# Equal slots for the heads' matrices in a hybrid conv and delta-rule step, with merged inverse levels and fewer last-token transposes

## The chip, the core and the metric

The kernel runs on one core of one Trainium2 chip. The metric is the device time of one execution in microseconds, and lower is better. A core has these engines, each working through its own queue of instructions in order: TensorE (PE in the profile, with its weight loads as PEld), VectorE (DVE), ScalarE (ACT), GpSimd (POOL), and SyncE (SP), which issues most of the DMA transfers. Engines wait for each other through semaphores. SBUF is the on-chip memory of 128 partitions, PSUM holds what TensorE writes.

## The reference

One layer of a hybrid decoder works on 1024 prompt tokens and 8 sample tokens, 1032 columns in all. A normalised input goes through one input projection; branch A is a short gated convolution, branch B a gated delta rule over 8 heads in chunks of 64 tokens; both are projected, merged by sigmoid gates, and go through an output projection. Outputs are the tokens, the last rows of both convolutions, and the heads' states.

```python
h = rmsnorm(x, norm_pre) * (1.0 + scale[:, None]) + shift[:, None]
proj = h @ w_in
hA, cA, bA, zA, qkv, zB, beta_raw, alpha_raw, gA, gB = jnp.split(proj, offs, axis=-1)
a_conv, new_buf_a = causal_dwconv(cA * hA, buf_a, conv_a_w)
yA = ((bA * a_conv) * jax.nn.silu(zA)) @ w_out_a
qkv_c, new_buf_b = causal_dwconv(qkv, buf_b, conv_b_w)
...
# per head and chunk: decay = exp(gc_i - gc_j), gc the running sum of log decays
a_mat = jnp.where(strict, jnp.einsum('bhncd,bhnsd->bhncs', kb, k) * decay, 0.0)
a_mat = a_mat + jnp.eye(C, dtype=jnp.float32)
sol = lax.linalg.triangular_solve(a_mat, rhs, left_side=True, lower=True, unit_diagonal=True)
...
def step(S, xs):
    v_new = u_c - jnp.einsum('bhcd,bhde->bhce', w_c, S)
    o = jnp.einsum('bhcd,bhde->bhce', qd_c, S) + jnp.einsum('bhcs,bhse->bhce', aqk_c, v_new)
    S = S * gl_c[..., None, None] + jnp.einsum('bhcd,bhce->bhde', kd_c, v_new)
    return S, o
...
merged = jax.nn.sigmoid(gA) * yA + jax.nn.sigmoid(gB) * yB
post = rmsnorm(merged @ w_o, norm_post)
y = (x + gate[:, None] * post).astype(x.dtype)
```

## The kernel before

Every large product is made in float32 by three matmuls on split operands: the high part of the input with the high part of the weights (xh,whi), the low part of the input (xl,whi), and the low part of the weights (xh,wlo). `run` walks a list of jobs. A **job** is one block of 128 columns of the input projection: three groups of 344 tokens, in each eight times three matmuls of 128x344, 72 in all. ScalarE makes the high part of a job's weights and VectorE the low part; an `evac` takes each group out of its accumulator. The order of the program is: the start-up (norm and modulation); the jobs of the heads (columns of K, Q and V, a gate and the gate zB for each head, then the remaining gates); `products`, which makes branch A's columns by a seven-product Strassen scheme (in the order P1, P2, P6, P7, P4, P5, P3) with matmuls of 128x258 columns, from operands (tiles qa, qb, q, thi, tlo) that VectorE builds ahead; `products_b`; the jobs of the output projections; and the tail with w_o.

The heads' delta rule runs in the gaps of the heads' jobs as **strands**, Python generators that `slot` steps between wide matmuls. A model of the clocks of all engines (`Sched`) decides at which wide matmul a strand's next piece is put in: `note` prices an instruction, `dma` a transfer, and a strand is stepped once the time of its last result lies `SLK` behind TensorE's modelled clock. What is decided there is the fixed order of each engine's queue. `Slots` is a pool of equal buffers (`T4`) with `get` and `give`; `ready` tells whether some are free, and strands wait by `yield` until they are.

A head passes these stages. `decay_gen` loads the head's running sums gc, broadcast to all partitions, into gcB, subtracts the token's own (DA), and forms two matrices of exponentials, DB for the inverse and DA for q by k. `delta_gen` then transposes k (`pa_t<-ident,kq`) into kd and sums its squares, does the same sums for q, multiplies k and q by k in split form (kqh, kql) into DB and DA, transposes v into vp, and scales q by the exponential of gcB. The kernel's chunks have 128 tokens, 8 in a head. The inverse of each chunk's 128x128 triangle is found in levels: its four diagonal blocks of 32 by VectorE in Tw (Ttmp; their layout is changed by way of DRAM, sA to At and sT to Tn), then the two halves of 64 one after the other (`Un,DB`, `Qs,Tn`, `Tn,Qs`), then the whole (`U,DB` and `Qs,T`). It is put together in U, one buffer that all heads share and that is cleared once. The **scan** goes over the chunks in order: `S,kq` on TensorE, X on VectorE, `X,U`, vn on ScalarE, `vn,kd` and `vn,DA`, then the new state S on VectorE. At the end the output `on` is normalised, transposed (`pa_t<-ident,on`) and gated by sz. `sample_gen` does the sample tokens (`qs_s,S`, matmuls of 128x2). `conv_state_gen` transposes the last tokens' rows of q, k, v (last_q, 24 tiles of 11 tokens) and of branch A (last_a, 8 tiles of 10) and stores them.

The buffers of `bp` (kq with 3, DA, DB, kd and vp with 2, gcB, Tw, Tn, Un, Qs, sz with 1) tie heads to each other: `decay_gen` of head h waits for head h-1's scaled q, and for the inverse and then the whole scan of head h-2; the inverse of head h waits for the scan of head h-1 because U is shared. All instructions are recorded through one helper, so their line is that of the helper (124 before, 134 after); they are told apart by tile names.

## Time and profile before

| what | value |
|---|---|
| time, median of three runs | 1429.38 us (1427.04 to 1431.44) |
| the profiled execution's own time | 1428.2 us |
| its span, first to last instruction | 1426.1 us |
| mean granted TensorE clock | 0.995 |
| bytes moved by DMA | 161.80 MB, 113 GB/s on average |
| the most frequent matmul, xh,whi of 128x344 and 128x512 columns | 1384 times, 453.4 us |
| TensorE waiting for DVE rx_y, in the start-up | 6.3 us, once |

The span holds all instructions; 2.1 us of the execution lie around it. In the profile's groups a row reads: line, engine, operation, output from inputs (partitions by elements), count, then busy time and the mean of one in ns. In the timeline a row reads: start, duration, engine, line, operation, and in brackets the idle time before it with its releaser. Matmuls are pipelined, so the durations of neighbours overlap; their pitch is the distance of the starts. Stages by time: start-up to about 80 us, the heads' jobs to 816 us, products and products_b after that, output projections and tail at the end.

### The profile page before, as it was taken

What the parts mean: (1) busy time and instruction counts of PE and PEld (TensorE: products, weight loads), DVE (VectorE), ACT (ScalarE), POOL (GpSimd) and SP (SyncE); (2) the same over time, 40 slices, a digit from 0 to 9 for tenths busy, and PEclk for the clock granted to TensorE, in tenths of its full rate; (3) what the DMA queues carried; (4) which work ended last, traced back from release to release, by engine and by line L of the source; (5) the groups of instructions that cost most, each with busy time, mean ns of one, the idle gap of its engine ahead of it and who ended that gap; (6) DMA issues with size and microseconds to landing.
All of it is one profiled execution on the core that took longest, in us unless ns stands there. A gap on an engine that the chain in (4) does not pass through costs nothing.

```text
span 1426.1 us, 26358 instructions
## 1 busy us (share of the span) xinstructions
PE 1394.4 (98%) x10274; PEld 1328.4 (93%) x10274; DVE 990.5 (69%) x2516; ACT 674.7 (47%) x1534; POOL 31.0 (2%) x72
## 2 busy tenths in 40 slices
PE   6999999999999999999999999999999999999997
PEld 4899998999989899998999999999999999999786
DVE  6766875697758768676463988877777787854553
ACT  6756744856466555747433433333333345432211
POOL 0000000000000000000000000000000110000000
PEclk9999999999999999999899999999999999999999
DMA  9622432153412423241332465432211876752321
GB/s 321 145 48 78 118 97 72 33 125 82 108 55 70 121 51 104 68 108 56 96 104 73 133 224 178 134 90 75 61 54 59 231 225 213 239 161 86 96 85 60
DMA packets 191591, 161.80 MB, mean 113 GB/s; under 512 B 34503, under 2 KB 167008, under 8 KB 191458
## 3 DMA queue, kind: packets, MB, share of 16 engines
q1 hardware_dynamic: 186912, 151.58, 36.0%
q0 software_dynamic: 4352, 8.46, 2.1%
q8 instruction: 81, 1.33, 0.4%
q14 instruction: 44, 0.36, 0.1%
q10 hardware_dynamic: 202, 0.08, 0.0%
HBM read 123.40 MB, written 36.91 MB: 112 GB/s over the span
## 4 chain that ended last, share of the span: by engine, by line
PE 78%; DVE 10%; DMA 6%; ACT 3%; issue 2%; SPq 1%; DVEq 0%; ACTq 0%
PE pm_t L124 53%; PE pa_t L124 23%; PE pb L124 2%; DVE wlo L124 1%; DVE Ttmp L124 1%; DVE Tw L124 1%; DMA At<-sA 1%; DVE acc L124 1%; SPq L124 1%; DMA xs<-in_x_prompt_dram 1%; DMA gcB<-gsc 1%; DVE on L124 1%; DVE mrg L124 1%; DVE vT L124 1%; DVE ro_a L124 0%
## 5 line engine op out<-in xcount | busy, mean ns | idle before, releaser
L124 PE MATMUL pm_t<-xh,whi 128*128 128x344 f32 (+1 forms) x1384 | 453.4, 328 | 0.0
L124 PE MATMUL pm_t<-xl,whi 128*128 128x344 f32 (+1 forms) x1384 | 436.2, 315 | 0.0
L124 PE MATMUL pm_t<-xh,wlo 128*128 128x344 f32 (+1 forms) x1384 | 435.8, 315 | 0.0
L124 PEld LDWEIGHTS pm_t<-xh,whi 128*128 128x128 f32 x1384 | 261.6, 189 | 1.6
L124 PEld LDWEIGHTS pm_t<-xl,whi 128*128 128x128 f32 x1384 | 261.8, 189 | 0.4
L124 PEld LDWEIGHTS pm_t<-xh,wlo 128*128 128x128 f32 x1384 | 261.2, 189 | 0.4
L124 ACT CAST whi<-wr 128x1024 fp32r<-128x1024 f32 x60 | 62.8, 1047 | 139.4 <-PE pm_t L124 65.7
L124 DVE TENSOR_TENSOR wlo<-wraw,whi 128x512 fp32r<-128x512 f32 x112 | 76.5, 688 | 35.6 <-ACT whi L124 35.1
L124 ACT CAST whi<-wraw 128x512 fp32r<-128x512 f32 x112 | 68.7, 624 | 55.8 <-PE pm_t L124 53.0
L124 PE MATMUL pm_t<-thi,wlo 128*128 128x258 f32 x304 | 86.3, 284 | 1.3 <-DVE wlo L124 1.2
L124 PE MATMUL pa_t<-thi,wlo 128*128 128x258 f32 x304 | 86.2, 284 | 0.1
L124 PE MATMUL pm_t<-tlo,whi 128*128 128x258 f32 x304 | 85.9, 283 | 0.0
L124 PE MATMUL pa_t<-tlo,whi 128*128 128x258 f32 x304 | 85.9, 283 | 0.0
L124 PE MATMUL pm_t<-thi,whi 128*128 128x258 f32 x304 | 85.8, 282 | 0.0
L124 PE MATMUL pa_t<-thi,whi 128*128 128x258 f32 x304 | 85.8, 282 | 0.0
L124 DVE TENSOR_TENSOR wlo<-wr,whi 128x1024 fp32r<-128x1024 f32 x60 | 73.2, 1220 | 10.3 <-ACT whi L124 10.1
L124 PE MATMUL pa_t<-xh,whi 128*128 128x258 f32 x256 | 72.4, 283 | 0.0
L124 PE MATMUL pa_t<-xh,wlo 128*128 128x258 f32 x256 | 72.2, 282 | 0.0
L124 PE MATMUL pa_t<-xl,whi 128*128 128x258 f32 x256 | 72.2, 282 | 0.0
L124 DVE SCALAR_TENSOR_TENSOR kq<-raw,vecs,kq 128x528 f32<-128x528 f32 x96 | 69.6, 761 | 2.4 <-ACT kq L124 2.4
L124 PE MATMUL pm_t<-ylo,whi 128*128 128x344 f32 x192 | 61.4, 321 | 0.6 <-DVE ylo L124 0.6
L124 PE MATMUL pm_t<-yhi,whi 128*128 128x344 f32 x192 | 61.4, 321 | 0.0
(397 smaller groups left out, 3065.5 us busy)
## 6 DMA issues: line engine op xcount, KB each, us to landing
wraw<-in_w_in_dram SPq DMA_DIRECT2D x48, 512.0 KB
wr<-in_w_in_dram SPq DMA_DIRECT2D x64, 256.0 KB
aw<-in_ada_w_dram SPq DMA_DIRECT2D x16, 512.0 KB
gBsc<-gate SPq DMA_DIRECT2D x8, 516.0 KB
gAsc<-gate SPq DMA_DIRECT2D x8, 516.0 KB
txs<-phi SPq DMA_DIRECT2D x8, 516.0 KB
txs<-plo SPq DMA_DIRECT2D x8, 516.0 KB
yAsc<-acc SPq DMA_DIRECT2D x8, 516.0 KB
```

The lines of the kernel that those rows point to most:

```text
L124: r = f(*args, **kw)
```

## The change

Buffers: T4 has 7 slots for 6, and 11 more ("hb") that live as long as `bp`. DB, DA, kd, gcB, the inverse's small tiles (Tw, Tn, Un and Qs in one slot, Ts) and sz now take slots; vp is written over vT, `on` over DA, and U over DB, whose other blocks POOL clears (`clear`, 24 memsets). A slot carries the modelled time at which it comes free, and `ready` counts only those whose time has come. A head's decay matrices no longer wait for the scan of head h-2, nor its inverse for the scan of head h-1; the scan alone waits for the scan before it.

Loads: the gc rows are loaded once into DA and a second time into gcB, for the scaled q, which a strand of its own (`qd_gen`) now makes. q's sums move behind the transposes of v.

Levels: the two halves of 64 go out in one step. Last tokens: last_q and last_a are stored with tokens outside and tiles inside, so that three transposes (72, 96 and 96 columns) and one (80) take the place of 24 and 8; stores are cut by token. The model: a transfer issued by SyncE costs 380 ns, arrives 800 behind, and one with short runs or a broadcast costs 4.7 times its size (`spread`).

```diff
-NT4 = 6
+NT4 = 7
+NHB = 11
...
+        t = max(self.clk[eng], self.cur.t if self.cur else self.clk["PE"]) + (380.0 if eng == "SY" and not self.cold else 60.0)
...
-        self.arrival = self.clk["DMA"] + 700.0
+        self.arrival = self.clk["DMA"] + 800.0
...
+def spread(out, in_):
+    a, b = ([d for d in x.ap if d[1] > 1] for x in (out, in_))
+    run = min(x[-1][1] if x and x[-1][0] == 1 else 1 for x in (a, b))
+    return 4.7 if run <= 32 or (b and b[0][0] == 0) else 1.0
...
         def ready(self, n=1):
-            return len(self.free) >= n
+            t = max(sched.clk["PE"], sched.cur.t if sched.cur else 0.0)
+            return sum(i[3] <= t for i in self.free) >= n
...
-        def give(self, v):
-            self.free.append(self.held.pop(id(v))[0])
+        def give(self, v, t=0.0):
+            i = self.held.pop(id(v))[0]
+            self.free.append(i[:3] + (max(t, sched.cur.t if sched.cur else 0.0),))
...
+    gc_rows = lambda h: gsc.rearrange("(c h) i -> h c i", h=NH)[h].unsqueeze(0).to_broadcast([P, NC, C])
...
     def decay_gen(h, st):
-        while not flags.get("ba") or (h and not flags.get(("qd", h - 1))) \
-                or (h > 1 and not flags.get(("inv", h - 2))):
-            yield
-        gcB = bp.tile([P, NC, C], F32, tag="gcB", name="gcB")
-        SY.dma_start(out=gcB, in_=gsc.rearrange("(c h) i -> h c i", h=NH)[h].unsqueeze(0).to_broadcast([P, NC, C]))
-        yield
-        while h > 1 and not flags.get(("done", h - 2)):
-            yield
-        DB = bp.tile([P, NC, C], F32, tag="DB", name="DB", bufs=2)
-        DA = bp.tile([P, NC, C], F32, tag="DA", name="DA", bufs=2)
+        yield from when(lambda: flags.get("ba") and (not h or flags.get((DEC, h - 1))), lambda: T4.ready(RDC))
+        DB_, DA_ = (T4.get(n_, S) for n_ in ("DB", "DA"))
+        DB, DA = (v.rearrange("p (c i) -> p c i", i=C) for v in (DB_, DA_))
+        SY.dma_start(out=DA, in_=gc_rows(h))
+        yield
         for c in range(NC):
-            act(DA[:, c, :], gcB[:, c, :], AF.Identity, bias=neg["gc"][:, c, h:h + 1])
+            act(DA[:, c, :], DA[:, c, :], AF.Identity, bias=neg["gc"][:, c, h:h + 1])
...
+        st.update(DB=DB, DA=DA, DB_=DB_, DA_=DA_)
...
+    def clear(v):
+        t = sched.cur.t
+        GP.memset(v, 0.0)
+        sched.cur.t, sched.cur.eng = t, None
+
+    def qd_gen(h, qd, gcB, t):
+        sched.at(t)
+        yield
         act(gcB, gcB, AF.Exp)
-        st.update(gcB=gcB, DB=DB, DA=DA)
+        yield
+        tt(qd, qd, gcB, ALU.mult)
+        T4.give(gcB)
+        flags[("qd", h)] = True
...
-        kq, vT, gcB, DB, DA = st["kq"], st["v"], st["gcB"], st["DB"], st["DA"]
+        yield from when(lambda: "DA" in st)
+        waiting.add(h)
+        yield from when(lambda: T4.ready(RDL - 1))
+        waiting.discard(h)
+        kq, vT, DB, DA = st["kq"], st["v"], st["DB"], st["DA"]
...
+        kd_, kh_, kl_ = (T4.get(n_, S) for n_ in ("kd", "kqh", "kql"))
+        kd, vp = (v.rearrange("p (c d) -> p c d", d=C) for v in (kd_, vT[:, 0:S]))
...
-        Tw = bp.tile([P, 8, 32], F32, tag="Tw", name="Tw")
+        Tw, Tn, Un = (Ts_[:, o:o + 256].rearrange("p (r j) -> p r j", j=32) for o in (0, 512, 768))
+        Qs = Ts_[:, 0:512].rearrange("p (c j) -> p c j", j=64)
...
-        T4.give(vT)
-        qd = kq[:, 1, 0:S]
-        tt(qd, qd, gcB.rearrange("p c i -> p (c i)"), ALU.mult)
-        flags[("qd", h)] = True
-        yield
+        yield from when(lambda: T4.ready())
+        gcB = T4.get("gcB", S)
+        sched.loose()
+        SY.dma_start(out=gcB.rearrange("p (c i) -> p c i", i=C), in_=gc_rows(h))
+        t_gc = sched.arrival
+        sched.loose(False)
+        yield from sums(1, ssq)
+        start(qd_gen(h, kq[:, 1, 0:S], gcB, t_gc))
...
+        U_, U = st["DB_"], DB
...
         yield
-        while h and not flags.get(("done", h - 1)):
-            yield
...
-        for p in range(2):
-            b1 = slice(64 * p, 64 * p + 32)
-            b2 = slice(64 * p + 32, 64 * p + 64)
-            pt = ps_aux().rearrange("p (c j) -> p c j", j=64)
+        B1, B2 = ([slice(64 * p + o, 64 * p + o + 32) for p in range(2)] for o in (0, 32))
+        pt = ps_aux().rearrange("p (c j) -> p c j", j=64)
+        for b1, b2 in zip(B1, B2):
             for c in range(NC):
                 PE.matmul(pt[b1, c, 0:32], lhsT=DB[b2, c, b1], rhs=Un[b2, c, :], start=True, stop=True)
+        sched.loose()
+        for b1 in B1:
             A.copy(out=Qs[b1, :, 0:32], in_=pt[b1, :, 0:32])
-            yield
-        for p in (0, 1):
-            b1 = slice(64 * p, 64 * p + 32)
-            b2 = slice(64 * p + 32, 64 * p + 64)
-            pt = ps_aux().rearrange("p (c j) -> p c j", j=64)
+        sched.join("A")
+        yield
+        for b1, b2 in zip(B1, B2):
+            clear(U[b2, :, b1])
+        pt, pt2 = (ps_aux().rearrange("p (c j) -> p c j", j=64) for _ in range(2))
+        for b1 in B1:
             for c in range(NC):
                 PE.matmul(pt[b1, c, 0:32], lhsT=Tn[b1, c, :], rhs=Qs[b1, c, 0:32], start=True, stop=True)
...
+        for c in range(NC):
+            PE.matmul(pt2[B2[0], c, 0:32], lhsT=Qs[B1[0], c, 0:32], rhs=Tn[B1[0], c, :], start=True, stop=True)
+        sched.loose()
+        A.copy(out=U[B1[1], :, B2[1]], in_=pt[B1[1], :, 0:32])
+        A.copy(out=U[B1[0], :, B2[0]], in_=pt[B1[0], :, 0:32])
+        A.copy(out=T11[B2[0], :, 0:32], in_=pt2[B2[0], :, 0:32])
+        sched.join("A")
...
-        flags[("inv", h)] = True
+        clear(U[64:128, :, 0:64])
...
-        while (h > 1 and not flags.get(("out", h - 2))) or not T4.ready():
-            yield
...
+        T4.give(Ts_)
+        flags[("inv", h)] = True
...
+
+        on_, on = st["DA_"], DA
+        yield from when(lambda: flags.get(("qd", h)) and (not h or flags.get(("done", h - 1))))
...
+        for v in (kd_, vT, U_):
+            T4.give(v)
...
-                st["szt"] = bp.tile([P, NT], F32, tag="sz", name="sz", bufs=1)
+                st["szt"] = T4.take("sz", NT)
...
+            src, nt, o_p, o_s, row, cuts = last_q, 24, n_conv_qkv_p, n_conv_qkv_s, 2, (0, 3, 7, 11)
...
-            for t0 in range(0, nt, 4):
-                pt = ps_aux()
-                for t in range(4):
-                    transpose(pt[:n, t * P:(t + 1) * P], src[:, t0 + t, :])
-                while not T4.ready():
-                    yield
...
+            src, nt, o_p, o_s, row, cuts = last_a, NK, n_conv_a_p, n_conv_a_s, 1, (0, 10)
+        flat, np_ = src.rearrange("p n t -> p (n t)"), cuts[-1] - NB
+        groups = list(enumerate(zip(cuts, cuts[1:])))
+        yield from when(lambda: T4.ready())
+        lq = T4.get("lq", 512)
+        pt = ps_aux()
+        for g, (a, b) in groups:
+            transpose(pt[:(b - a) * nt, g * P:(g + 1) * P], flat[:, a * nt:b * nt])
...
+            if a == 0:
+                store(o_p[0, 0].rearrange("n (t d) -> (n t) d", d=P), v[:np_ * nt])
+            for n in range(max(a, np_), b):
+                store(o_s[0, n - np_, row].rearrange("(t d) -> t d", d=P), v[(n - a) * nt:(n - a + 1) * nt])
+        T4.give(lq)
```

TensorE, about the end of head 6's inverse, where before the inverse meets the last-token transposes (S_8211 is a sample state, T_ the assembled inverse; Qs and Tn belong to the halves of 64):

```order
L124 MATMUL pa_t<-ident,last_q 11x128 x4
L124 MATMUL pa_t<-Qs,Tn 32x32 x8
L124 MATMUL pa_t<-Tn,Qs 32x32 x8
L124 MATMUL pm_t<-xh,wlo 128x344
L124 MATMUL pa_t<-qs_s,S_8211 128x2 x8
L124 MATMUL pm_t<-xh,whi 128x344
L124 MATMUL pm_t<-xl,whi 128x344
L124 MATMUL pm_t<-xh,wlo 128x344
L124 MATMUL pm_t<-xh,whi 128x344
L124 MATMUL pa_t<-ident,last_q 11x128 x4
L124 MATMUL pa_t<-Qs,Tn 32x32 x8
L124 MATMUL pa_t<-ident,last_q 11x128 x4
```

Four wide matmuls in a row are the most that stand there between small groups (of four transposes, eight 32x32 or eight 128x2 matmuls). After the change the last-token transposes are gone from there. The sparsest place is now another one, 42.1 jobs into the heads' stage, where the last head's vT and the output of the head before (DA) are transposed beside the samples' matmuls:

```order
L134 MATMUL pa_t<-ident,vT 128x128 x4
L134 MATMUL pa_t<-qs_s,S_8425 128x2 x4
L134 MATMUL pm_t<-xh,whi 128x344
L134 MATMUL pm_t<-xl,whi 128x344
L134 MATMUL pm_t<-xh,wlo 128x344
L134 MATMUL pa_t<-ident,DA 128x128 x4
L134 MATMUL pa_t<-S,kq 128x128 x2
L134 MATMUL pa_t<-qs_s,S_8425 128x2 x4
L134 MATMUL pm_t<-xh,whi 128x344
L134 MATMUL pm_t<-xl,whi 128x344
L134 MATMUL pm_t<-xh,wlo 128x344
L134 MATMUL pa_t<-ident,vT 128x128 x4
```

Transposes come in fours there, with three wide matmuls between groups.

TensorE, one round of the last head's scan, with U before:

```order
L124 MATMUL pa_t<-S,kq 128x128 x2
L124 MATMUL pm_t<-xh,whi 128x344
L124 MATMUL pm_t<-xl,whi 128x344
L124 MATMUL pm_t<-xh,wlo 128x344
L124 MATMUL pa_t<-X,U 128x128
L124 MATMUL pm_t<-xh,whi 128x344
L124 MATMUL pm_t<-xl,whi 128x344
L124 MATMUL pm_t<-xh,wlo 128x344
L124 MATMUL pm_t<-xh,whi 128x344
L124 MATMUL pm_t<-xl,whi 128x344
L124 MATMUL pm_t<-xh,wlo 128x344
L124 MATMUL pa_t<-vn,kd 128x128
```

and with the inverse in DB after:

```order
L134 MATMUL pa_t<-S,kq 128x128 x2
L134 MATMUL pm_t<-xh,wlo 128x344
L134 MATMUL pm_t<-xh,whi 128x344
L134 MATMUL pa_t<-X,DB 128x128
L134 MATMUL pm_t<-xl,whi 128x344
L134 MATMUL pm_t<-xh,wlo 128x344
L134 MATMUL pm_t<-xh,whi 128x344
L134 MATMUL pa_t<-vn,kd 128x128
L134 MATMUL pa_t<-vn,DA 128x128
```

Three and six wide matmuls stood between the links of the scan, now there are two and three. From the last head's output transposes to the products' first matmul of 128x258 there were 186 rows of TensorE's queue, now 121. In the heads' stage the stream of wide matmuls is broken by small work 325 times before, 298 times after.

VectorE, at the end of the last head, where the products' operands begin (ro_y is the norm's factor, vecs_83 a weight, q_ a block of an operand). Before:

```order
L124 TENSOR_TENSOR on<-on,ro_y 128x1024
L124 SCALAR_TENSOR_TENSOR on<-pa_t,vecs_83,sz 128x512 x2
L124 TENSOR_TENSOR qa<-xh,xl 128x1032
L124 TENSOR_TENSOR qb<-xh,xl 128x1032
L124 TENSOR_TENSOR q_9569<-qa 128x516
L124 TENSOR_TENSOR qa<-xh,xl 128x1032
L124 TENSOR_TENSOR qa<-qb,qa 128x516
```

and after:

```order
L134 TENSOR_TENSOR DA<-DA,ro_y 128x1024
L134 TENSOR_TENSOR qa<-xh,xl 128x1032
L134 SCALAR_TENSOR_TENSOR DA<-pa_t,vecs_83,sz 128x512 x2
L134 TENSOR_TENSOR qb<-xh,xl 128x1032
L134 TENSOR_TENSOR q_9506<-qa 128x516
L134 TENSOR_TENSOR qa<-xh,xl 128x1032
L134 TENSOR_TENSOR qa<-qb,qa 128x516
```

The order of the builds is the same, with one qa ahead of the output's last step; what changes is how far behind them the products start on TensorE. Ahead of the weights of P6 VectorE's queue now ends with these rows:

```order
L134 TENSOR_TENSOR wsum<-wr 128x1024
L134 TENSOR_TENSOR tlo<-qa,thi 128x516
L134 TENSOR_TENSOR wr<-wr 128x1024
L134 TENSOR_TENSOR acc<-pa_t,acc 128x258
L134 TENSOR_TENSOR wr<-wsum,wr 128x1024
L134 TENSOR_TENSOR acc<-pa_t,acc 128x258
L134 TENSOR_TENSOR wr<-wr 128x1024
L134 TENSOR_TENSOR acc<-pa_t,acc 128x258
L134 TENSOR_TENSOR wlo<-wr,whi 128x1024
```

Before, two plo rows and two xl rows stood ahead of those weights (`wlo<-wr,whi`) too; they come later now.

More of the change, by code (lines that the diff above doesn't have):

```diff
@@ L45 @@
 SG = 0
+DEC = "qd"
+RDL = 4
+RDC = 2
 FILL = (1, 1, 1, 1, 1, 1, 1, 1)
@@ L249, in hybrid_step @@
     hist_a = cpool.tile([P, NK, 2 * NB], F32, name="hist_a")
-    last_q = cpool.tile([P, 24, 11], F32, name="last_q")
-    last_a = cpool.tile([P, NK, 10], F32, name="last_a")
+    last_q = cpool.tile([P, 11, 24], F32, name="last_q")
+    last_a = cpool.tile([P, 10, NK], F32, name="last_a")
     wba = cpool.tile([P, NK, 16], F32, name="wba")
@@ L651, in extend @@
         def extend(self, pool, tag, n, width):
-            self.free += [(pool, f"{tag}{i}", width) for i in range(n)]
+            self.free += [(pool, f"{tag}{i}", width, 0.0) for i in range(n)]
         def ready(self, n=1):
-            return len(self.free) >= n
+            t = max(sched.clk["PE"], sched.cur.t if sched.cur else 0.0)
+            return sum(i[3] <= t for i in self.free) >= n
         def take(self, name, w):
@@ L661, in get @@
         def get(self, name, w):
-            i = min((i for i in self.free if i[2] >= w), key=lambda i: i[2])
+            t = max(sched.clk["PE"], sched.cur.t if sched.cur else 0.0)
+            i = min((i for i in self.free if i[2] >= w), key=lambda i: (i[3] > t, ("hb" in i[1]) == (name in LATE), i[2], i[3]))
             self.free.remove(i)
+            if sched.cur:
+                sched.cur.t = max(sched.cur.t, i[3])
             t = i[0].tile([P, i[2]], F32, tag=i[1], name=name)
@@ L887, in delta_gen @@
         ch = lambda a: a[:, :, h:h + 1]
-        while "DA" not in st or "v" not in st or (h > 1 and not flags.get(("done", h - 2))):
-            yield
-        kq, vT, gcB, DB, DA = st["kq"], st["v"], st["gcB"], st["DB"], st["DA"]
+        yield from when(lambda: "DA" in st)
[3 more added lines that the diff above has]
+        kq, vT, DB, DA = st["kq"], st["v"], st["DB"], st["DA"]
         V.tensor_copy(out=qs_s[:, h, :, 0], in_=smpl(kq[:, 0, :]))
@@ L928, in delta_gen @@
         for half in range(2):
-            while not T4.ready(2):
-                yield
-            kh_, kl_ = T4.get("kqh", S), T4.get("kql", S)
+            if half:
+                T4.give(kh_)
+                T4.give(kl_)
+                kh_, kl_ = T4.get("kqh", S), T4.get("kql", S)
             kh, kl = (v.bitcast(F32R).rearrange("p (s i) -> p s i", s=2) for v in (kh_, kl_))
@@ L947, in delta_gen @@
                 yield
-            T4.give(kh_)
-            T4.give(kl_)
+        T4.give(kh_)
+        T4.give(kl_)
+        At_, Ts_ = T4.get("At", S), T4.get("Ts", S)
         sched.join("V")
@@ L1231, in sample_gen @@
     def sample_gen(h):
-        while not flags.get(("qs", h)) or (h and not flags.get(("smp", h - 1))) or not T4.ready(2):
+        while not flags.get(("qs", h)) or (h and not flags.get(("smp", h - 1))) or not T4.ready(2 + 4 * len(waiting)):
             yield
@@ L1316, in conv_state_gen @@
             SY.dma_start(out=n_conv_qkv_s[0, :, 0:2, :], in_=state_conv_qkv[0, :, 1:3, :])
[L1317 removed]
+            src, nt, o_p, o_s, row, cuts = last_q, 24, n_conv_qkv_p, n_conv_qkv_s, 2, (0, 3, 7, 11)
         else:
             SY.dma_start(out=n_conv_a_s[0, :, 0, :], in_=state_conv_a[0, :, 1, :])
[L1320 to L1334 removed]
+            src, nt, o_p, o_s, row, cuts = last_a, NK, n_conv_a_p, n_conv_a_s, 1, (0, 10)
[6 more added lines that the diff above has]
+            transpose(pt[:(b - a) * nt, g * P:(g + 1) * P], flat[:, a * nt:b * nt])
+        sched.loose()
+        for g, (a, b) in groups:
+            A.copy(out=lq[:(b - a) * nt, g * P:(g + 1) * P], in_=pt[:(b - a) * nt, g * P:(g + 1) * P])
+        sched.join("A")
+        yield
+        for g, (a, b) in groups:
+            v = lq[:, g * P:(g + 1) * P]
+            if a == 0:
[3 more added lines that the diff above has]
+        T4.give(lq)
     def rowgate_gen():
@@ L1701, in to_products @@
         drain_bg()
+        T4.free = [i for i in T4.free if i[0] is not bp]
         bp.release()
```

79 lines of the change are left out of this document (24 added, 55 removed).

## The prediction, made before the changed kernel ran

> **What bounds the kernel now.** I read the page first: the engines' totals, the granted clock and the chain that ended last.
>
> ```profile
> PE 1394.4 (98%) x10274; PEld 1328.4 (93%) x10274; DVE 990.5 (69%) x2516; ACT 674.7 (47%) x1534; POOL 31.0 (2%) x72
> PEclk9999999999999999999899999999999999999999
> PE 78%; DVE 10%; DMA 6%; ACT 3%; issue 2%; SPq 1%; DVEq 0%; ACTq 0%
> ```
>
> TensorE is busy in 98% of the span; nothing else is near it. So only three things can shorten this kernel: fewer matmul instructions, TensorE's idle time, and its clock, which one slice shows below 9. Next come the waits of TensorE (the views' columns: who waits for what, us in total, times, longest) and three stages by windows (PE, PEld, DVE, ACT, POOL busy, granted clock, DMA share, GB/s).
>
> ```profile
> PE pb L124 <- DVE rx_y L124: 6.3, 1, 6.3
> ...
> PE pa_t L124 <- DVE X L124: 2.5, 4, 1.3
> PE pa_t L124 <- DVE on L124: 2.2, 6, 0.6
> PE pa_t L124 <- DVE kd L124: 1.5, 1, 1.5
> ...
> PE pa_t L124 <- ACT vn L124: 1.2, 2, 0.6
> ...
> PE pa_t L124 <- DVE S L124: 0.8, 2, 0.4
> ```
>
> ```profile
> 80.00:120.00 40.00, 38.53 (x254) 38.14 (x252) 22.42 (x65) 29.59 (x76) 0.41 (x2) 1.00 0.32 69
> 400.00:500.00 100.00, 97.08 (x731) 91.79 (x731) 68.38 (x224) 64.17 (x179) 2.50 (x5) 1.00 0.30 78
> 1000.00:1100.00 100.00, 100.00 (x837) 100.00 (x836) 73.39 (x123) 29.53 (x40) 0.00 (x0) 1.00 0.21 59
> ```
>
> The largest wait (rx_y) is in the start-up, which the diff leaves alone. In the products TensorE has no gap at all; in the heads' stage (80 to 816 us) it loses 3 us in 100, at its start 1.5 in 40. What the heads cause in waits is 2.5 + 2.2 + 1.5 + 1.2 + 0.8 = 8.2 us. The clock's one dip there, cut at its own edges:
>
> ```profile
> 676.88:680.29 3.41, 3.41 (x51) 3.31 (x48) 0.51 (x4) 2.73 (x11) 0.00 (x0) 1.00 0.03 7
> 680.29:690.53 10.24, 10.24 (x65) 8.62 (x63) 3.18 (x8) 3.32 (x6) 0.00 (x0) 0.50 0.22 55
> 690.53:693.90 3.37, 3.37 (x31) 3.26 (x31) 0.86 (x4) 0.58 (x1) 0.00 (x0) 1.00 0.01 1
> ```
>
> For 10.24 us the clock was granted at 0.50, after 3.41 us in which PE was busy throughout but with small work: head 6's inverse, the last-token transposes and the 128x2 sample products. It costs 10.24 x 0.5 = 5.1 us.
>
> **The change part by part.** The sum is made against the profiled execution's own time, 1428.2 us (span 1426.1 and 2.1 around it); the median of the three runs, 1429.4, is 1.2 above it.
>
> *Fewer transposes.* 24 + 8 last-token transposes become 3 + 1.
>
> ```profile
> 300.10 0.61 PE L124 MATMUL pa_t<-S,kq 128*128 128x128 f32 x4
> 300.46 0.40 PE L124 MATMUL pm_t<-xh,whi 128*128 128x344 f32 x1
> 300.70 0.32 PE L124 MATMUL pm_t<-xl,whi 128*128 128x344 f32 x1
> 300.86 0.32 PE L124 MATMUL pm_t<-xh,wlo 128*128 128x344 f32 x1
> 666.59 0.60 PE L124 MATMUL pa_t<-ident,last_q 128*11 128x128 f32 x4
> ```
>
> ```profile
> L124 PE MATMUL pa_t<-ident,last_a 128*10 128x128 f32 x8 | 1.2, 272 | 0.0
> ```
>
> Four of them take 0.60 us and a single one 0.27, so each after the first adds (0.60 - 0.27)/3 = 0.11 us. 28 fewer: **-3.1**. The wide transposes move the same 128 columns and get the same price. Wide matmuls follow each other at 0.16 us; the first after small work starts its successor 0.24 later (300.46 to 300.70), so each break in the wide stream costs 0.08. In the two orders the breaks in the heads' stage go from 325 to 298, by the transposes and the merged levels: 27 x 0.083 = **-2.2**. Both are on TensorE, which is the bound, so nothing hides them.
>
> *The clock.* The cluster of the dip is gone from the order: without last-token transposes, and with two levels in one step, wide matmuls stand between all small groups of head 6. I take **-5.1**. The other end is 0: the order has another sparse place (42.1 jobs into the stage; 24 transposes and 8 sample products among nine wide matmuls), and no row tells how sparse is too sparse. The trace shows one dip among eight heads, so a single such place more often passes than not; so I take the gain.
>
> TensorE was busy in 3.41 of the 3.41 us before the fall. The Trainium skill (TensorE: Matmul & The Clock Gate, "HAM oscillation") asks for no idle gap over about 3.4 us; here the clock fell without one, and the trace decides. The Trainium skill says on the same page ("Part 4: PE-mode transpose") that transposes do not count as busy in the same way. By that rule the place at 42.1 drops the clock too and this term is 0, the sum 5.1 higher; rival B has that outcome.
>
> *The first head.* Its kd wait (1.5) stands behind the first load of gc rows:
>
> ```profile
> 91.25 8.89 DMA gcB<-gsc
> ```
>
> In the new order head 0's kq transposes come 0.3 to 0.8 jobs later, and a job is 72 x 0.157 = 11.3 us, so 3 to 9 us more slack: **-1.5** (bounds 0 and -1.5).
>
> *Scan waits.* More slots let a head's matrices live beside the next head's; heads 0 to 6 get more wide matmuls between X, vn and S. Bounds: 0 and the 2.5 + 2.2 + 1.2 + 0.8 = 6.7 of the rows above. I take **-2**: the waits are seldom (14 in eight heads), come from DVE's queue more than from the order, and DVE's work is not less (2191 rows before, 2199 now).
>
> *The last head's scan.* Here the order is tighter, not looser. A link's least time, from matmul to dependent matmul, by the last head before:
>
> ```profile
> 755.77 0.61 PE L124 MATMUL pa_t<-S,kq 128*128 128x128 f32 x4
> 756.19 0.35 DVE L124 SCALAR_TENSOR_TENSOR X<-pa_t,nx,vp 128x128 f32<-128x128 f32 x1 [0.79 <-PE pa_t L124]
> 756.60 0.49 PE L124 MATMUL pa_t<-X,U 128*128 128x128 f32 x2
> 757.12 0.27 ACT L124 COPY vn<-pa_t 128x128 f32<-128x128 f32 x1 [1.25 <-PE pa_t L124]
> 757.44 0.49 PE L124 MATMUL pa_t<-vn,kd 128*128 128x128 f32 x2
> ```
>
> S,kq to X,U 0.83; X,U to vn,kd 0.84. Two or three wide matmuls (0.08 + 3 x 0.16 + the small work's own 0.25, 0.8 at most) stand between them now; before, mostly three to six. About 21 links short by 0.1 each would be 2.1, less where three stand; the inverse's levels, two to five wide matmuls apart, add 0.4. **+2** (bounds 0 and 4).
>
> *From the heads to the products.* The last head ends later in the stream, so VectorE starts the products' operands later.
>
> ```profile
> 784.77 1.23 DVE L124 TENSOR_TENSOR on<-on,ro_y 128x1024 f32<-128x1024 f32 x1
> ...
> 788.19 1.23 DVE L124 TENSOR_TENSOR qa<-xh,xl 128x1032 f32<-128x1032 f32 x1
> 789.34 1.23 DVE L124 TENSOR_TENSOR qb<-xh,xl 128x1032 f32<-128x1032 f32 x1
> 790.49 0.69 DVE L124 TENSOR_TENSOR q<-qa 128x516 f32<-128x516 f32 x1
> 791.10 1.23 DVE L124 TENSOR_TENSOR qa<-xh,xl 128x1032 f32<-128x1032 f32 x1
> ...
> 823.43 0.43 DVE L124 TENSOR_TENSOR acc<-pa_t,acc 128x258 f32<-128x258 f32 x1
> 823.78 1.21 DVE L124 TENSOR_TENSOR wlo<-wr,whi 128x1024 fp32r<-128x1024 f32 x1
> ```
>
> ```profile
> 816.05 0.28 PE L124 MATMUL pm_t<-xh,whi 128*128 128x258 f32 x1
> ...
> 827.53 0.28 PE L124 MATMUL pm_t<-thi,whi 128*128 128x258 f32 x1
> ```
>
> From the end of on's multiply (786.0) to the products' first matmul (816.05) lie 30.05 us and 186 rows of TensorE, 0.162 a row. Now 121 rows lie there: 19.6 us. P6 (the third product) starts 11.5 us later, 31.1 after VectorE may begin. Until the weights' low part of P6 VectorE then has 8 rows of 128x1032 and 7 of 128x1024 at a pitch of 1.15, 24 of 128x516 at 0.61, three acc at 0.35 and the last head's output at 1.41: 17.3 + 14.6 + 1.1 + 1.4 = 34.3 us. TensorE waits the difference, 3.2; part of the 0.4 is pipelining, so **+2.8**. Before, the same weights were done at 825.0, 2.5 us early. Bounds 0 (other rows of VectorE come later) and 5 (the plo and xl rows of 1.15 that now stand behind P6's weights press on P4's).
>
> *At nothing.* In place of one clear of U at the start there are 24 on POOL; it is busy for 31.0 of 1426 us, and nothing on TensorE's path waits for it in the trace. The second load of gc rows falls on DMA engines that are 0.30 busy, and the stores of the last rows are waited for by nobody. What it costs if the load's cover is gone is rival E.
>
> Sum: -3.1 - 2.2 - 5.1 - 1.5 - 2 + 2 + 2.8 = -9.1, so 1428.2 - 9.1 = 1419.1: **1419**.
>
> **The rivals.**
>
> *B, the clock falls all the same.* For it: the place at 42.1 jobs, and that the one dip of before came in a place like it. Against it: the mix differs (no 32x32 matmuls). 1419 + 5.1 = **1424**.
>
> *C, the crowded end weighs more, with the clock down.* The scan of the last head waits 4, products 5: 1424 + 2 + 2.2 = **1428**. For it: the last head's rows stand closer than any of before. Against it: in all eight heads of before TensorE waited for X four times, 1.3 us at the longest.
>
> *D, the slots free more.* All the 6.7 of the heads' waits and only half of the +4.8 at the end: 1419 - 4.7 - 2.4 = **1412**.
>
> *E, slower: a load heads ScalarE's queue.* gcB is loaded a second time in each head, and its exp stands on ScalarE ahead of other strands' evacuations.
>
> ```profile
> ACT DA L124 <- DMA gcB<-gsc: 4.6, 2, 3.8
> ```
>
> Before, one such wait lasted 3.8 us and did not reach TensorE, for ScalarE had slack there. If the load now lands 4 us late in every head, ScalarE stands for 3.8; the four small accumulators fill in about half of it, and TensorE waits the other 2: 8 x 2 = 16 on the forecast's 1419, and with even odds of one dip of the clock 2.5 more: **1437**. It decides once the load takes over about 2 us longer than the order's model allows. That model now gives 512 KB / 360 x 4.7 = 6.8 us and 1.9 around it, 8.7; the trace has 8.9, at a DMA share of 0.32 in that stretch (0.30 between 400 and 500 us), which speaks against it.
>
> *F, the change doesn't do what it says* (levels or transposes left apart): excluded, since the rows of the two orders stand in the section on the change.
>
> **How the numbers follow.** A 0.42, B 0.25, C 0.13, D 0.10, E 0.10. The forecast is A's 1419. The range takes A, B and C with their bounds, half of D and the near end of E: 1411 to 1431. A measurement of this kernel tells about 0.3% (4.3 us) from no change. Faster than 1425.1: A, D and about half of B's spread around 1424 (0.14): 0.66. Slower than 1433.7: E, 0.10. The rest, 0.24, is the same.
>
> **What would show it.** The windows of the heads' stage: no granted clock under 1 in A, 10.24 us of 0.50 in B, and where. TensorE's waits: no kd at about 113 us; wlo of 2 to 3 us some 11.5 us behind the first 128x258 matmul; X, vn and S in the last head only, about 2 us in all. ScalarE's waits: `gcB` behind its load, under 2 us each in A, near 4 and with TensorE waiting on pa_t in E. Wrong would be: TensorE waiting over 5 us in products, any wait behind POOL's clears, or a busy time of TensorE that falls by more than 5.1 + 5.3 us or less than 5.3.

## The result, and the profile after

The changed kernel takes **1465.88 us** (median of four, 1462.73 to 1469.08) where the kernel before takes 1430.31 in the same runs: a ratio of **1.0253** (1.0221 to 1.0285). It is slower by 36 us; 1419 with a range of 1411 to 1431 was predicted. The profiled execution has 1469.1 us and a span of 1467.4.

The page of the kernel after, its totals, clock and chain:

```profile
PE 1407.9 (96%) x10246; PEld 1348.8 (92%) x10246; DVE 996.9 (68%) x2516; ACT 677.1 (46%) x1534; POOL 38.0 (3%) x95
...
PEclk9999999999998897999999999999999999999999
...
PE 81%; DMA 9%; ACT 4%; DVE 4%; issue 1%; SPq 1%; DVEq 0%; ACTq 0%
PE pm_t L134 55%; PE pa_t L134 24%; DMA DA<-gsc 3%; DMA gcB<-gsc 2%; PE pb L134 2%; DMA yraw<-yAsc 1%; ACT L134 1%; ACT whi L134 1%; DMA xs<-in_x_prompt_dram 1%; SPq L134 1%; DMA gAsc<-gate 1%; ACT DA L134 0%; DMA sg<-gBsc 0%; DVE kq L134 0%; DVE wlo L134 0%
```

Both halves of the loss stand in the first row. TensorE's time without work, span less busy time, goes from 31.7 to 59.5 us (+27.8), and its busy time from 1394.4 to 1407.9 (+13.5) although it has fewer instructions: the clock. The clock's records show half clock for 68.3 us in all, in nine stretches (between 85 us and the last 20), against one of 10.24 before. Half of that time is lost at the most, so busy time less half of it is an estimate of the work at full clock: 1389.3 before, 1373.7 after. The lower clock costs up to 29 us of busy time, and some 16 of them are made up by work that the change takes out. These figures are of one execution each, and the clock of one program varies: the mean granted clock of the kernel before is 0.988 to 0.997 in its executions (0.995 in the profiled one), which is 13 us of time or 26 us of half clock; that of the changed kernel, 0.974 to 0.977, lies clear below. In the chain, DA<-gsc is new with 3%, and gcB<-gsc has 2% where it had 1%. Waits of TensorE after, from 85 to 815 us (who waits for what, us, times, longest):

```profile
PE pa_t L134 <- ACT vn L134: 15.7, 4, 7.3
PE pa_t L134 <- issue: 5.4, 1, 5.4
PE pa_t L134 <- ACT Ts L134: 5.1, 2, 3.8
PE pa_t L134 <- ACT DB L134: 4.0, 2, 3.3
PE pm_t L134 <- ACT raw L134: 3.3, 1, 3.3
```

33.5 us in ten waits, 28.1 of them for ScalarE, at different tiles (the one put down to `issue` ends at 466.61, just behind ScalarE's copy of Ts). An engine that makes others late at unrelated tiles is itself held by something, so its own waits come next:

```profile
ACT DA L134 <- DMA DA<-gsc: 36.3, 8, 6.4
...
ACT gcB L134 <- DMA gcB<-gsc: 14.3, 3, 6.6
ACT L134 <- DMA gcB<-gsc: 12.5, 3, 5.5
```

(The row without a tile is the load of ScalarE's table ahead of gcB's exponential.) Fourteen of the sixteen loads of gc rows were waited for, 63.1 us in all, 4.5 a time. From issue to use they took 8.1 to 13.1 us, one of them 17.4. One of them, on three engines: SyncE's issue, then ScalarE, then TensorE (start, duration; in brackets the idle time before).

```profile
402.93 0.37 SPq L134 DMA_DIRECT2D DA<-gsc  x1
```

```profile
406.95 0.31 ACT L134 COPY DA<-pa_t 128x128 f32<-128x128 f32 x1
407.11 0.33 ACT L134 ACTIVATE junk<-pa_t 128x128 f32<-128x128 f32 x1
...
412.33 2.44 ACT L134 ACTIVATE DA<-DA,ngc 128x128 f32<-128x128 f32 x8 [4.80 <-DMA DA<-gsc]
414.68 0.24 ACT L134 COPY vn<-pa_t 128x128 f32<-128x128 f32 x1
```

```profile
409.57 0.38 PE L134 MATMUL pa_t<-X,DB 128*128 128x128 f32 x2
...
414.97 0.80 PE L134 MATMUL pa_t<-vn,kd 128*128 128x128 f32 x2 [4.54 <-ACT vn L134]
```

ScalarE is done with other work at 407.5, takes up the next head's subtraction and stands until the load, issued at 402.93, has landed at 412.3. Behind it in the queue stands the scan's vn, whose operand was ready just after 409.57; TensorE, too, has vn,kd next in its queue, so wide matmuls that could fill the time stand behind that. Windows on this wait and behind it (PE, PEld, DVE, ACT, POOL busy, clock, DMA):

```profile
410.43:414.97 4.54, 0.01 (x1) 0.00 (x0) 0.62 (x2) 2.64 (x10) 0.20 (x1) 0.90 0.78 239
414.10:420.93 6.83, 5.96 (x23) 5.96 (x24) 3.72 (x10) 4.77 (x11) 0.00 (x0) 0.50 0.03 11
420.93:424.30 3.37, 3.37 (x26) 3.36 (x25) 2.15 (x8) 2.97 (x5) 0.00 (x0) 1.00 0.60 156
```

The 4.54 us without work are followed by half clock: 5.96 us of work that would take about 3.3 at full clock, for wide matmuls follow each other at 0.29 us there and at 0.16 before the wait. This wait is paid about one and a half times. In the kernel before the same load was far ahead of its use, for it went into a buffer of its own while `decay_gen` still waited for the scan of two heads ago:

```profile
531.45 0.38 SPq L124 DMA_DIRECT2D gcB<-gsc  x1
```

```profile
572.93 2.44 ACT L124 ACTIVATE DA<-gcB,ngc 128x128 f32<-128x128 f32 x8
```

41 us lie between issue and use there; from the third head on it is 27 to 71 us, and only the first two heads use it some 9 us behind the issue. The change loads into the slot that is to be worked in, once it is free, and uses it at once.

### The profile page after: what moved, and what is told of

Same layout as the page of the kernel before. It is cut to its first block, busy times and chain, and to the rows that moved or that the text cites. A ratio compares the mean times of both kernels' runs of the same rounds, so it can differ in the third digit from the quotient of the medians.

```text
span 1467.4 us, 26409 instructions
## 1 busy us (share of the span) xinstructions
PE 1407.9 (96%) x10246; PEld 1348.8 (92%) x10246; DVE 996.9 (68%) x2516; ACT 677.1 (46%) x1534; POOL 38.0 (3%) x95
## 3 DMA queue, kind: packets, MB, share of 16 engines
q1 hardware_dynamic: 195592, 155.77, 36.3%
## 4 chain that ended last, share of the span: by engine, by line
PE 81%; DMA 9%; ACT 4%; DVE 4%; issue 1%; SPq 1%; DVEq 0%; ACTq 0%
PE pm_t L134 55%; PE pa_t L134 24%; DMA DA<-gsc 3%; DMA gcB<-gsc 2%; PE pb L134 2%; DMA yraw<-yAsc 1%; ACT L134 1%; ACT whi L134 1%; DMA xs<-in_x_prompt_dram 1%; SPq L134 1%; DMA gAsc<-gate 1%; ACT DA L134 0%; DMA sg<-gBsc 0%; DVE kq L134 0%; DVE wlo L134 0%
## 5 line engine op out<-in xcount | busy, mean ns | idle before, releaser
L134 PEld LDWEIGHTS pm_t<-xh,whi 128*128 128x128 f32 x1384 | 265.3, 192 | 5.0 <-ACT raw L134 3.5
L134 PEld LDWEIGHTS pm_t<-xl,whi 128*128 128x128 f32 x1384 | 265.2, 192 | 0.2
L134 PEld LDWEIGHTS pm_t<-xh,wlo 128*128 128x128 f32 x1384 | 264.8, 191 | 0.2
L134 ACT ACT_TABLE_LOAD x41 | 52.6, 1283 | 33.2 <-DMA gcB<-gsc 12.5
```

The costliest lines, as they stand in the source:

```text
L134: r = f(*args, **kw)
```

## The experiments

The theory: the loads of gc rows land behind the moment at which ScalarE takes up their users, and block it. Rivals: the merged levels and the tighter order stall TensorE (waits for Ts, DB, vn); or the clock falls by itself in sparse places. PE idle is span less busy time of the profiled execution; half clock is the sum of the clock's records of 0.50 between 85 us and the last 20. Ratios are to the kernel before in the same runs; its medians there are 1428.0 to 1431.9, so differences of a few us between rows are better read from the ratios. The last three columns are of one execution each, with the spread of the clock told above.

| kernel | us | ratio (interval) | PE busy | PE idle | half clock |
|---|---|---|---|---|---|
| before | 1430.3 | 1 | 1394.4 | 31.7 | 10.2 |
| after | 1465.9 | 1.0253 (1.0221 to 1.0285) | 1407.9 | 59.5 | 68.3 |
| pin_both | 1451.8 | 1.0169 (1.0144 to 1.0195) | 1398.3 | 49.0 | 44.4 |
| contig | 1415.7 | 0.9912 (0.9894 to 0.9931) | 1385.4 | 31.6 | 23.9 |
| contig_pin | 1420.0 | 0.9942 (0.9923 to 0.9960) | 1384.6 | 33.2 | 13.7 |
| contig_gc | 1443.6 | 1.0097 (1.0061 to 1.0134) | 1391.6 | 48.0 | 34.1 |
| contig_da | 1443.9 | 1.0108 (1.0082 to 1.0134) | 1393.9 | 47.0 | 41.0 |
| before_da | 1479.2 | 1.0339 (1.0309 to 1.0369) | 1423.2 | 58.3 | 68.3 |
| before_contig | 1423.5 | 0.9950 (0.9927 to 0.9973) | 1399.6 | 25.2 | 27.3 |
| before_last | 1423.8 | 0.9968 (0.9953 to 0.9984) | 1393.6 | 28.3 | 17.1 |
| contig_nolast | 1427.2 | 0.9979 (0.9959 to 0.9999) | 1390.6 | 36.9 | 34.1 |
| contig_unmerge | 1436.0 | 1.0030 (1.0013 to 1.0047) | 1397.9 | 39.0 | 37.6 |
| after_oldmodel | 1453.2 | 1.0156 (1.0130 to 1.0181) | 1398.3 | 58.3 | 54.6 |
| contig_oldmodel | 1406.4 | 0.9833 (0.9807 to 0.9859) | 1375.6 | 31.3 | 0 |

### Holding the users back: pin_both

```diff
-            act(DA[:, c, :], DA[:, c, :], AF.Identity, bias=neg["gc"][:, c, h:h + 1])
+            r = act(DA[:, c, :], DA[:, c, :], AF.Identity, bias=neg["gc"][:, c, h:h + 1])
+            if c == 0:
+                tc.keep_in_program_order(r)
...
-        act(gcB, gcB, AF.Exp)
+        tc.keep_in_program_order(act(gcB, gcB, AF.Exp))
```

> The changed kernel, with two kinds of ScalarE instructions held behind everything that the program writes ahead of them for ScalarE: the first subtraction on DA and the exponential of gcB, the two that wait for the loads of gc rows. Nothing is left out. Load theory (both stand in ScalarE's queue before their load has landed, and what stands behind them, vn, raw, Ts and DB, keeps TensorE waiting): ScalarE's waits for the two loads fall from 36.3 + 14.3 + 12.5 us to under 10, TensorE's waits in the heads' stage from 33.5 to under 10, and at most one stretch of half clock is left there; 1420 to 1432 us. First rival (the merged levels and the crowded order stall TensorE, the loads are bystanders): waits for Ts and DB stay, 1455 us or more. Second rival (the clock falls by sparse work alone): the idle time goes, the half clock stays, about 1440.

1451.8 us, between the theories. ScalarE's waits in this kernel:

```profile
ACT DA L134 <- DMA DA<-gsc: 45.6, 8, 10.6
```

gcB's waits, 26.8 us, are gone, and 14 us with them. DA's have grown: the subtraction is still taken up 2 to 9 us behind its load's issue. That the instruction written ahead of it runs early too is my reading. So this edit tried half of what was meant; the other half needs loads that land sooner.

### Loads that land sooner: contig, contig_pin

```diff
-        transpose(pt[:64, 0:C], gcf)
+        gch = ap_.tile([P, NH, NC], F32, name="gch")
+        V.tensor_copy(out=gch, in_=gc.rearrange("p c h -> p h c"))
+        transpose(pt[:64, 0:C], gch.rearrange("p h c -> p (h c)"))
...
-    gc_rows = lambda h: gsc.rearrange("(c h) i -> h c i", h=NH)[h].unsqueeze(0).to_broadcast([P, NC, C])
+    gc_rows = lambda h: gsc.rearrange("(h c) i -> h c i", h=NH)[h].unsqueeze(0).to_broadcast([P, NC, C])
```

> The changed kernel, with the scratch of gc rows laid out by head, so that a load reads one run of 4 KB for a partition in place of eight of 512 bytes; one small copy of 128x64 is added ahead. The bytes of each load stay 512 KB, and no wait or place in a queue is touched by hand. Load theory, with the load's time set by its count of packets: it lands in about 5 us in place of 9 to 10, ScalarE's waits for it fall from 63 us to under 20, 1425 to 1440 us. Load theory, with the load's time set by its bytes: no change, 1460 to 1470. Rival (merged levels and order): no change either, but also with loads that land sooner.

> Both edits together: rows laid out by head, and the two kinds of instructions held behind what is written ahead of them. Load theory: within 4 us of the better one of the two, since either alone takes the wait away; 1418 to 1430. Rival (order and levels): 1455 or more.

1415.7 us: better than expected by any theory, and faster than the kernel before. All parts of the change are still in it. One load in contig's chain of waits, and all that ScalarE still waits for loads:

```profile
567.59 3.87 DMA gcB<-gsc
```

```profile
ACT DA L134 <- DMA DA<-gsc: 5.7, 3, 3.0
...
ACT gcB L134 <- DMA gcB<-gsc: 0.8, 1, 0.8
```

This load of 512 KB lands in 3.9 us, the one at 402.93 above in 9.3. Loads differ with the traffic beside them: the four that ScalarE waited for here took 3.9 to 8.2 us from issue to use, against the 8.1 to 13.1 and once 17.4 above, and the first head's load, issued at 91 us in both, was used at 99.86 there after a wait and at 96.13 here without one. The waits fall from 63.1 to 6.5 us, and TensorE's idle time is back to 31.6. Levels and slots are as in the changed kernel, and the stalls are gone. The order is not: the sixteen loads leave in another sequence (with D for DA and G for gcB, DGGDDGDGDGDGDDGG in the changed kernel, DGGDDGDDGGDDGGDG here), and only about a fifth of ScalarE's rows stand in the same order in both. So this run alone doesn't tell shorter loads from another order; the next two and after_oldmodel with contig_oldmodel do. With the pins added nothing more is won (1420.0).

### Which load: contig_gc, contig_da

A second scratch laid out by head is read by one of the two loads only.

```diff
+        SY.dma_start(out=gsd, in_=gcd)
...
-        SY.dma_start(out=gcB.rearrange("p (c i) -> p c i", i=C), in_=gc_rows(h))
+        SY.dma_start(out=gcB.rearrange("p (c i) -> p c i", i=C), in_=gd_rows(h))
```

> The changed kernel with a second scratch laid out by head, read by the second load (gcB) alone; the first load (DA) keeps its runs of 512 bytes. Holding gcB's exponential back took 14 us off and left 45.6 us of waits for DA. Theory (both loads block ScalarE, the first, which the change moved to just ahead of its use, more than the second, which it added): gcB's waits vanish, DA's 36 to 46 us stay, 1440 to 1455 us. Rival (the added load is the whole cost): 1416 to 1422.

> The counterpart of the kernel with only gcB's loads in runs of 4 KB: here DA's loads alone are short, gcB's keep 512 bytes. So far: both long 1465.9, gcB's short 1443.6, both short 1415.7 us. If the two costs add, DA's short alone gives 1465.9 - 1443.6 + 1415.7 = 1438, and the waits left are gcB's, 15 to 25 us on ScalarE. If one long load in a head is enough to bring the clock down: 1445 or more. If the load that the change moved to its use is the greater part: 1430 or less.

1443.6 and 1443.9 us. Against the changed kernel either load alone, made short, takes 22 us off, both take 50. The order of work is contig's in both (98% or more of ScalarE's rows), so contig is the cleaner comparison: either load, made long again, costs 28 us. What ScalarE still waits, contig_gc first:

```profile
ACT DA L134 <- DMA DA<-gsc: 37.3, 8, 6.6
```

```profile
ACT gcB L134 <- DMA gcB<-gsc: 20.6, 6, 6.3
```

So the load that the change added costs as much as the one that it moved to its use, though ScalarE waits longer for the moved one; the two nearly add, 44 of the 50. The added load is not the whole cost, and neither is the moved one.

### The fault put into the kernel before: before_da

```diff
         DA = bp.tile([P, NC, C], F32, tag="DA", name="DA", bufs=2)
+        SY.dma_start(out=DA, in_=gsc.rearrange("(c h) i -> h c i", h=NH)[h].unsqueeze(0).to_broadcast([P, NC, C]))
+        yield
...
-            act(DA[:, c, :], gcB[:, c, :], AF.Identity, bias=neg["gc"][:, c, h:h + 1])
+            act(DA[:, c, :], DA[:, c, :], AF.Identity, bias=neg["gc"][:, c, h:h + 1])
```

> The kernel before with one thing of the change put in: the gc rows are loaded a second time for each head, into DA itself and only once DA comes free, and the subtraction works in place; gcB is loaded early as before for the scaled q. No slots, no merged levels, no other order. Theory (a load into the buffer that its user waits for is in nobody's shadow, since the user stands in ScalarE's queue before it has landed): ScalarE waits 3 to 6 us for DA's load in most of the eight heads, TensorE 10 or more in all, the clock falls behind some of these waits; 1440 to 1460 us. Rival (the slots, the merged levels and the order make the stalls): 1427 to 1432.

1479.2 us, 47 slower than before, with no slots and no merged levels:

```profile
ACT DA L124 <- DMA DA<-gsc: 42.3, 7, 9.0
...
ACT L124 <- DMA gcB<-gsc: 29.7, 6, 9.3
```

Here, too, both loads are waited for, not only the one put in. gcB is issued where it was, but its exponential no longer shares a buffer with the subtraction, and ScalarE takes it up earlier. In the third head:

```profile
209.50 1.06 ACT L124 ACTIVATE gcB<-gcB 128x1024 f32<-128x1024 f32 x1
```

```profile
275.25 1.57 ACT L124 ACTIVATE DA<-DA,ngc 128x128 f32<-128x128 f32 x5 [4.50 <-DMA DA<-gsc]
```

The program writes the exponential behind this subtraction; it runs 66 us ahead of it, and 10 us behind its own load's issue (199.30). The idle time (58.3) and the half clock (68.3) of the changed kernel come with this one edit, so slots and merged levels are not needed for the loss. The order of work shifts with the edit, too (about 40% of ScalarE's rows stand in the same order as before); that the loads make the loss is read from the waits.

### The layout in the kernel before: before_contig

The edit of contig, in the kernel before.

> The kernel before with gc rows laid out by head and nothing else. Its loads are issued long before their use from the second head on, so by the theory only the first head's wait for kd (1.5 us) and what ScalarE loses there can be won: 1425 to 1429 where the kernel before has 1428 to 1430. Rival (shorter loads help every transfer beside them): 1420 or less; then the gain of the changed kernel with this layout would not be the change's own.

1423.5 us, 1.5 below the expected range and above the rival's 1420. Idle time falls by 6.5 us, more than the first head's wait; why TensorE's waits for X and vn are gone too was not followed up. By the ratios, the change is worth 0.9912 / 0.9950 = 0.996 where both have short loads: 5 to 6 us, by the two intervals 1 to 10, where 9.1 were forecast.

### Parts of the change: before_last, contig_nolast, contig_unmerge

before_last puts the last-token part alone into the kernel before; contig_nolast takes it out of contig; contig_unmerge has the halves of 64 one after the other again:

```diff
-        for b1, b2 in zip(B1, B2):
-            for c in range(NC):
-                PE.matmul(pt[b1, c, 0:32], lhsT=DB[b2, c, b1], rhs=Un[b2, c, :], start=True, stop=True)
+        for p in range(2):
+            b1 = slice(64 * p, 64 * p + 32)
+            b2 = slice(64 * p + 32, 64 * p + 64)
+            pt = ps_aux().rearrange("p (c j) -> p c j", j=64)
+            for c in range(NC):
+                PE.matmul(pt[b1, c, 0:32], lhsT=DB[b2, c, b1], rhs=Un[b2, c, :], start=True, stop=True)
...
+            yield
```

> The kernel before with the last-token part of the change alone (three and one wide transposes for 24 and 8, last_q and last_a stored with tokens outside). By the prediction's terms: 28 transposes fewer, 3.1 us, and some 5 to 8 breaks of the wide stream fewer, 0.5 us; with the half-clock stretch of head 6 gone 5.1 more, so 1420 to 1422 where the kernel before has 1429 to 1430. If the stretch stays or moves: 1425 to 1427. If the transposes hid in time that TensorE had anyway: 1429.

> The changed kernel with gc rows laid out by head, and the last-token part of the change undone (24 and 8 transposes again). By the prediction's price of 3.1 us for the transposes and some 0.5 for breaks: 1419 to 1421 where it has 1415.7 with them. If the transposes also bring the clock down: 1424 to 1429. If other small work fills in: 1416.

> The changed kernel with gc rows laid out by head and the two halves of 64 taken apart again, one after the other as before. By the prediction's price for a break in the wide stream, 0.083 us, some 16 breaks more: 1.3 us slower, 1416 to 1418. If the merged step is what brings the clock down at 196.7 and 749.6 us (10.24 + 6.83 us at half clock): up to 8 us faster, 1408 to 1412. If its longer chain delays the heads: 1420 or more.

The last-token part is worth 4.6 us in the kernel before (0.0032 of 1428.7) and 11.5 in contig (10 by the ratios). In the kernel before TensorE's busy time falls by 0.8 us while half clock grows by 6.8, that is 3.4 of loss: an estimate of 4.2 of work gone, where 3.6 was reckoned. In contig it is idle time (36.9 to 31.6) and clock (34.1 to 23.9); by the same estimate no work is gone there. Here the clock's part is not of one execution only: the mean granted clock is 0.990 to 0.994 in contig's executions, 0.986 to 0.993 in contig_nolast's and 0.985 to 0.992 in contig_unmerge's. Taking the merged step apart costs 20 us (17 by the ratios): 7.4 of idle time and 12.5 of busy time, with 13.7 us more of half clock. That is far beyond 1.3 for the breaks; the expectation named a delayed chain as the third outcome, and the clock goes the wrong way for the second. Under half of ScalarE's rows stand in contig's order there, so how much of it is the merged step itself stays open.

### The order's charges: after_oldmodel, contig_oldmodel

```diff
-        t = max(self.clk[eng], self.cur.t if self.cur else self.clk["PE"]) + (380.0 if eng == "SY" and not self.cold else 60.0)
+        t = max(self.clk[eng], self.cur.t if self.cur else self.clk["PE"]) + 60.0
...
-        self.arrival = self.clk["DMA"] + 800.0
+        self.arrival = self.clk["DMA"] + 700.0
...
-                s.dma(n, 4 * size * out.shape[0] * spread(out, kw["in_"]))
+                s.dma(n, 4 * size * out.shape[0])
```

> The changed kernel with gc rows laid out by head, and the order's model charging transfers as before the change (60, 700, no factor for short runs or broadcasts). Theory (where ScalarE's instructions stand is settled when the framework orders the queues by its own reckoning, and the kernel's model only sets the order in which the program writes them): within 5 us of 1415.7. Rival (the new charges keep the loads' users back): waits behind loads come back, 1425 or more.

> The changed kernel with its transfers charged as before the change, gc rows in runs of 512 bytes as changed. With short loads the old charges were worth 9 us. Theory (both loads still take 9 to 10 us, and the framework puts their users where it takes them to have landed): waits for the two loads stay near 60 us on ScalarE; 1445 to 1470. Rival (the new charges are what put the users ahead of their loads): 1425 or less.

With long loads 1453.2, with short ones **1406.4 us**. In these two the sixteen loads leave in the same sequence and 98% of ScalarE's rows stand in the same order, so the 47 us between them are the loads': ScalarE's waits for them are 54.4 us in the one and 10.6 in the other. 1406.4 is the fastest of all, 1.7% below the kernel before and 9 below contig, where the theory had said within 5. The new charges, meant to hold users back until their loads have landed, are worth nothing for that: without them the waits for loads are 54.4 us (30.0, 19.7 and 4.7) in place of 63.1, and the time is 13 us less. The page of contig_oldmodel:

```profile
PE 1375.6 (98%) x10246; PEld 1321.8 (94%) x10246; DVE 989.4 (70%) x2517; ACT 675.6 (48%) x1532; POOL 40.7 (3%) x95
```

Idle time is as in contig (31.3 to 31.6); the 9 us are busy time, and contig's three stretches of half clock are gone (mean granted clock 0.998 to 0.999 in all executions). Why the charges change little at the loads shows in ScalarE's instructions in the changed kernel, in the first head:

```profile
119.60 1.06 ACT L134 ACTIVATE gcB<-gcB 128x1024 f32<-128x1024 f32 x1 [6.63 <-DMA gcB<-gsc]
120.56 0.26 ACT L134 ACTIVATE junk<-pa_t 128x128 f32<-128x128 f32 x1
```

The program writes gcB's exponential behind all sums of that head (`qd_gen` is started after `sums(1, ssq)`), yet it stands ahead of the first of them (junk). With the exponential of before_da, 66 us ahead of its place, this shows that the queue is ordered again after the program has written it. That the framework takes loads for shorter than they are is my reading of this and of the 4.5 us by which users are early; its reckoning itself was not looked at.

## Why the prediction was wrong, point by point

**The step that failed** is the one that put the loads at nothing, and with them the weight of rival E. It held 8.9 us of load against 8.7 in the order's model, "which speaks against it". The comparison was right and proved nothing: where ScalarE's instruction stands is not set by that model (after_oldmodel, and the order above). Eleven of the fourteen loads that were waited for took less than 2 us over those 8.7, the lateness from which E was to decide, and ScalarE waited all the same, for it took up their users 3 to 9 us behind the issue (once 15). E also named only the added load; the load that the change moved from 41 us ahead of its use to a few us ahead was read as a mere rename of its buffer. The diff showed it: one line writes the load's target as DA, and the wait that used to stand between load and use is gone. E's mechanism, ScalarE blocked at the head of its queue, was right; its size was not: 16 us of waits and 2.5 of clock were reckoned; 27.8 of idle time and up to 29 of clock were measured. The loss is 36 us and not their sum because the change also takes out work, 14 to 16 us of TensorE's time at full clock by the estimate above (1389.3 before, 1373.5 in contig, 1375.6 in contig_oldmodel), where the sum had 5.3.

**The clock (-5.1)** was wrong even with short loads: the old dip at 680 us is gone, but contig has others, three with 23.9 us. The forecast rested on one execution with one dip, and other executions of the same kernel had a lower clock. One of contig's dips is in the first head's inverse:

```profile
193.30:196.70 3.40, 3.40 (x64) 2.96 (x63) 0.00 (x0) 1.20 (x4) 0.00 (x0) 1.00 0.02 5
196.70:206.90 10.20, 10.20 (x57) 9.59 (x56) 5.39 (x13) 4.94 (x10) 0.53 (x1) 0.50 0.07 14
```

Again TensorE is busy throughout, here with the levels and the 128x2 sample products between them, as at 680 us before. In contig_oldmodel, where the two lie apart in the first head (182 to 185 and 213 to 228 us), no clock falls. But the mixture is not the rule: in contig samples stand between the levels from 510.9 to 525 us too and the clock stays full, and its fall at 749.6 us comes behind the last head's levels with no samples beside them and no wait of TensorE. What brings the clock down there is open. The third fall, at 783.8, begins in the wait for the gate told below. The place that rival B feared, 42.1 jobs into the stage with its transposes, kept the full clock in the changed kernel:

```profile
743.40:750.20 6.80, 6.64 (x55) 6.27 (x53) 3.73 (x11) 3.68 (x4) 0.00 (x0) 1.00 0.80 218
```

So the rule that transposes do not count as busy, weighed in the prediction (the Trainium skill, TensorE: Matmul & The Clock Gate, "Part 4: PE-mode transpose"), is not borne out at this place: vT, DA, the samples and two links of the scan stand there, and no half clock follows.

**Transposes and breaks (-5.3)**: the transposes hold in the kernel before (4.2 estimated against 3.6 in before_last), but in contig what they win is idle time and clock. Taking the merging back cost 17 to 20 us in contig, more than its breaks, but with another order of work.

**The first head (-1.5)** holds: no wait for kd is left. **Scan waits (-2)** hold in contig: 4.0 us (DA 2.9, vn 0.7, S 0.2, junk 0.2) against 6.7. **The last head's scan (+2)** did not come: contig shows no wait of TensorE there, from 754 to 779 us.

**Heads to products (+2.8)**: the start was right. VectorE takes up qa at 832.02, 19.75 us ahead of the first 128x258 matmul at 851.77 (19.6 forecast); but TensorE waits 0.85 for P6's weights, and for their high part, by ScalarE, not the 2.8 for the low part. In contig another wait stands at this place, which no step named:

```profile
786.34 1.49 ACT L134 COPY gate<-pm_t 128x344 f32<-128x344 f32 x4 [9.09 <-DMA yBsc<-DA]
```

```profile
786.84 0.66 PE L134 MATMUL pm_t<-xh,whi 128*128 128x344 f32 x1 [4.37 <-ACT gate L134]
```

The last head's output now lies in a slot of `bp`, and the buffers that follow in that memory wait until its store is through. This is a price of the slots, 4.4 us, with the half clock behind it; in contig_oldmodel TensorE waits 0.4 for this tile, so the order decides whether it is paid.

## What to carry to other kernels

Where a change writes a load's result into the buffer that is worked in, look for the lead that goes with it: the time from issue to use in the trace before, against the load's own duration. An instruction that waits for a load at the head of an in-order queue stops all that stands behind it, and here the waits on TensorE's path were paid again by its clock. Before moving instructions to hide a load, make it shorter: the layout of the scratch was worth 47 us here with the order kept, while the dearer charges in the kernel's model lost 9 to 14.

## What the runs showed of the hardware

Loads of 512 KB, broadcast to 128 partitions, took 8.1 to 13.1 us (once 17.4) in runs of 512 bytes and 3.9 to 8.2 in runs of 4 KB where ScalarE waited for them, with 14,336 packets less in sixteen loads (195,592 to 181,256 on SyncE's queue). The Trainium skill (DMA: Bandwidth & Descriptors, "Specifications") gives 512 bytes as the least transfer for full rate; here runs of exactly that size took about twice as long as runs of 4 KB, and the measurement decides. These loads all read the same few rows; loads of distinct rows were not tried.

In the changed kernel each of the nine stretches of half clock begins in or just behind a wait of TensorE: seven at waits of 3.1 to 7.3 us (4.54 us, then 6.83 at 0.50), one at 2.2 us, one at 1.06 and 0.76 close together. The Trainium skill (TensorE: Matmul & The Clock Gate, "What's actually happening") says so of an idle window of about 3.4 us; here shorter waits had it too, and the measurement decides. Half clock also came without a wait, at 680 us before and at 196.7 and 749.6 us in contig.
